# Longer rows for the high part of the residual: eight tiles at eight places in SBUF

## The chip, the cores and the metric

The kernel runs on one core of one Trainium2 chip. The metric is the device time of one execution in microseconds (us). The times of before and after are medians over several runs; a profile is taken of one execution. The engines are called as in the profile: PE is TensorE (PEld its weight loads), DVE is VectorE, ACT is ScalarE, POOL is GpSimd, SP is SyncE, which issues most DMAs.

## The reference

The reference is a trunk of two encoder layers on a sequence of 512 tokens of 1024 channels, all in float32. Cut to what matters:

```
for i in range(2):
    proj = x @ w_in[i]                        # (512, 1024) @ (1024, 5120)
    qa, ka, va, qb, kb, vb, gl = split(proj)
    oa = banded_attention(rope(qa), rope(ka), va, sink)          # window 128
    ob = mix of three dilated_attention(rope(qb), rope(kb), vb)  # dilations 1, 4, 16
    ga, gb = split(sigmoid(gl + b_gate))
    h = (ga * (oa @ w_branch_a) + gb * (ob @ w_branch_b)) @ w_out
    x = layer_norm(ALPHA * x + h)
    mlp = relu(x @ w_up) ** 2 @ w_down        # 1024 -> 4096 -> 1024
    ple = sigmoid(x @ w_ple_gate + b) * (p[i] @ w_ple)
    x = layer_norm(ALPHA * x + mlp + ple)
```

## The kernel before

The residual x lies transposed in SBUF for the whole program: channels on the 128 partitions, in eight tiles (k = 0 to 7) of 128 channels by 512 tokens. A float32 value is kept as two parts of the type float32r: a high part, made by ScalarE with a cast, and a low part, the rest, made by VectorE with a subtraction. For x these are the tiles xhi and xlo. Weights are split in the same way into whi and wlo (bhi and blo where a set is held longer, dhi and dlo in the down projection), after they were fetched to wst by DMA. A product of two such numbers is three matmuls (high by high, low by high, high by low), which add up in one bank of PSUM:

```
        def mm3(ps, w, i, x, start, stop, part=False):
            s = slice(i * P, (i + 1) * P)
            nc.tensor.matmul(ps, w[0][:, s], x[0], ...)    # L308: stationary whi, moving xhi
            nc.tensor.matmul(ps, w[0][:, s], x[1], ...)    # L309: stationary whi, moving xlo
            nc.tensor.matmul(ps, w[1][:, s], x[0], ...)    # L310: stationary wlo, moving xhi
```

The tile named first behind the arrow in a row of the profile is the moving operand, the one that is streamed through the array, 512 columns at most; the second is the stationary one, which a weight load has put there. mm3t (L314 to L316) is the same with the roles changed: 128 tokens of x are stationary, 512 columns of weights move.

Two lines make the residual's tiles, in the pool cp, which is the first on the left side of SBUF:

```
        xhi = cp.tile([P, KT, S], F32R, name="xhi")
        xlo = cp.tile([P, KT, S], F32R, name="xlo")
        X = [(xhi[:, k, :], xlo[:, k, :]) for k in range(KT)]
```

Each layer goes through these stages. The attention stage projects x by w_in, block after block of 128 output channels (8 tiles x 3 matmuls by mm3 each; start is the first four blocks together, in the second layer partly in halves of 256 tokens), and puts the small matmuls of attention between them: scores (sa L509, sb L504), transposes of the probabilities (pta, ptb, L472), sums over values (oa, ob, L513 and L514). A forecast in the program sets the order of TensorE's work there; elsewhere it is the order in which the code is written. The mixer's outputs go through gates, the branch projections (ya, yb) and the output projection (wo). Then come the layer norm, the transposes back (xTn L1032), and new xhi and xlo: ScalarE writes xhi at L1041, VectorE reads it at L1043 to make xlo. The gate of the embedding (pg) uses mm3t with x as the stationary operand. The up projection (ps_up) makes 32 blocks of 128 by mm3 from all eight tiles, in four quarters; between the quarters stands the down projection (dn L1156), which reads hidden activations and weights, not x. A second layer norm closes the layer.

xhi is read by TensorE in the projections by w_in, in the up projection (L308, L310, moving) and in the gate of the embedding (L314, L315, stationary). The tiles of the left pools stand behind xhi in SBUF: xlo and small vectors in cp, weights in wp, then, one after another, the attention stage's pool av, the pool yp of the layer's result y, and the pools np and qp. Pools of the right side (rp, hp, wb, rg) are laid out from the other end.

Of the kernel before, what the change touches and what calls it, by code (L numbers as in the profile page):

```python
# [11 lines left out]
F32R = mybir.dt.float32r  # L12
# [9 lines left out]
P = 128  # L22
S = 512
D = 1024
KT = 8
# [197 lines left out]
def build(nc, tc, plan, down, xT, xN, pT, wst, vec, rows, sink, cst, out):  # L223
# [3 lines left out]
    with ctx:  # L227
        cp = ctx.enter_context(tc.tile_pool(name="cp", bufs=1))
# [132 lines left out]
            return pss  # L361


        xhi = cp.tile([P, KT, S], F32R, name="xhi")
        xlo = cp.tile([P, KT, S], F32R, name="xlo")
        X = [(xhi[:, k, :], xlo[:, k, :]) for k in range(KT)]

# [1178 lines left out]
```

## Time and profile before

| what | value |
|---|---|
| median of 3 runs | 1506.17 us (1505.03 to 1506.38) |
| the profiled execution | 1504.93 us |
| its span, first to last instruction | 1503.2 us |
| granted TensorE clock | 0.998 |
| TensorE busy, matmuls | 1491.1 us (99%), 7242 |
| VectorE busy | 1044.7 us (69%) |
| ScalarE busy | 762.4 us (51%) |
| GpSimd busy | 255.1 us (17%) |

Shares are of the span. A busy time counts an instruction from its start to its end, and matmuls overlap, so a share of 99% says that TensorE hardly ever stands still, and nothing about how fast it goes while it works. That is read from the distance between the starts of neighbouring matmuls, in the rows in order of time.

### The profile page before, as it was taken

To read this page: it belongs to the slowest core of one execution; us is meant where nothing else is said; L and a number is where in the kernel's file an instruction comes from. 1 tells how busy PE (TensorE), PEld (TensorE's weight loads), DVE (VectorE), ACT (ScalarE), POOL (GpSimd) and SP (SyncE) were. 2 spreads that over 40 slices of the span, in tenths; PEclk is the share of its full clock that TensorE was granted. 3 is DMA by queue.
4 is the path that set the end of the run, shared out by engine and by line. 5 is a ranking of instruction groups with operands and counts; after the bars stand their busy time and mean duration, and the time that the engine had idled before them with its cause. 6 is when DMAs were issued, how large, how long until landed. Compare 5 with 4: busy or idle time off the path is not lost.

```text
span 1503.2 us, 19458 instructions
## 1 busy us (share of the span) xinstructions
PE 1491.1 (99%) x7242; PEld 1241.0 (83%) x7242; DVE 1044.7 (69%) x1796; ACT 762.4 (51%) x1256; POOL 255.1 (17%) x216
## 2 busy tenths in 40 slices
PE   9999999999999999999999999999999999999997
PEld 7888888888888888888888888888888888888886
DVE  6766675458577677677877666754685867777778
ACT  5777774344344443434458777643442544444344
POOL 1212211110021110213012122102100202111121
PEclk9999999999999999999999999999999999999999
DMA  7656564555523414142366666546755233241402
GB/s 263 151 135 153 136 160 124 186 160 154 182 60 94 127 57 154 42 141 84 97 203 140 141 148 143 152 135 167 239 153 182 70 113 112 84 127 54 139 18 70
DMA packets 58894, 197.41 MB, mean 131 GB/s; under 512 B 7440, under 2 KB 7984, under 8 KB 58800
## 3 DMA queue, kind: packets, MB, share of 16 engines
q1 hardware_dynamic: 47552, 159.08, 33.1%
q0 software_dynamic: 10256, 36.70, 13.2%
q8 instruction: 56, 0.92, 0.2%
q10 hardware_dynamic: 992, 0.39, 0.1%
q14 instruction: 38, 0.31, 0.1%
HBM read 161.46 MB, written 6.37 MB: 112 GB/s over the span
## 4 chain that ended last, share of the span: by engine, by line
PE 92%; DVE 4%; ACT 1%; DMA 1%; issue 0%; POOL 0%; SPq 0%; DVEq 0%; POOLq 0%; ACTq 0%
PE dn L1156 19%; PE ps_up L310 8%; PE ps_up L309 8%; PE ps_up L308 8%; PE wo L316 2%; PE wo L314 2%; PE wo L315 2%; PE pg L314 2%; PE pg L315 2%; PE pg L316 2%; PE sa L509 1%; PE pta L472 1%; PE sb L504 1%; PE ya L308 1%; PE ya L309 1%; PE ya L310 1%
## 5 line engine op out<-in xcount | busy, mean ns | idle before, releaser
L249 ACT CAST whi<-wst 128x1024 fp32r<-128x1024 f32 (+2 forms) x120 | 121.2, 1010 | 252.2 <-PE ps_up L309 102.7
L250 DVE TENSOR_TENSOR wlo<-wst,whi 128x1024 fp32r<-128x1024 f32 (+2 forms) x120 | 149.2, 1248 | 100.8 <-ACT whi L249 99.6
L1119 POOL TENSOR_TENSOR hr<-r 128x512 f32<-128x512 f32 x64 | 108.8, 1701 | 547.4 <-ACT r L1111 516.1
L310 PE MATMUL ps_up<-xhi,wlo 128*128 128x512 f32 x512 | 199.5, 390 | 0.0
L308 PE MATMUL ps_up<-xhi,whi 128*128 128x512 f32 x512 | 199.4, 390 | 0.0
L309 PE MATMUL ps_up<-xlo,whi 128*128 128x512 f32 x512 | 199.4, 390 | 0.0
L309 PEld LDWEIGHTS ps_up<-xlo,whi 128*128 128x128 f32 x512 | 96.2, 188 | 19.9
L308 PEld LDWEIGHTS ps_up<-xhi,whi 128*128 128x128 f32 x512 | 96.1, 188 | 19.9
L310 PEld LDWEIGHTS ps_up<-xhi,wlo 128*128 128x128 f32 x512 | 96.2, 188 | 19.9
L1172 DVE TENSOR_TENSOR y<-y,dn 128x512 f32<-128x512 f32 (+1 forms) x98 | 65.9, 672 | 62.9 <-PE dn L1156 62.8
L249 ACT CAST whi<-raw 128x1024 fp32r<-128x1024 f32 x56 | 58.0, 1053 | 96.0 <-PE ps_up L309 57.7
L249 ACT CAST dhi<-raw 128x1024 fp32r<-128x1024 f32 x56 | 58.6, 1050 | 85.9 <-PE dn L1156 57.3
L256 POOL DMA_DIRECT2D wlo<-wst x54 | 47.3, 876 | 246.0 <-ACT wlo L255 151.9
L1099 DVE TENSOR_TENSOR raw<-raw,raw 128x1024 f32<-128x1024 f32 x64 | 84.7, 1324 | 0.3
L250 DVE TENSOR_TENSOR wlo<-raw,whi 128x1024 fp32r<-128x1024 f32 x56 | 68.3, 1220 | 14.1 <-ACT whi L249 14.1
L254 ACT CAST whi<-wst 128x1024 fp32r<-128x1024 f32 x54 | 56.5, 1047 | 32.3 <-PE ps_start L309 4.3
L250 DVE TENSOR_TENSOR dlo<-raw,dhi 128x1024 fp32r<-128x1024 f32 x56 | 68.9, 1239 | 3.6 <-ACT dhi L249 3.6
L255 ACT ACTIVATE wlo<-whi 128x1024 fp32r<-128x1024 f32 x54 | 57.3, 1061 | 0.9
L1156 PE MATMUL dn<-wlo,smh 128*128 128x512 f32 (+1 forms) x130 | 51.1, 393 | 0.2
L1130 DVE TENSOR_TENSOR sml<-sr,smh 128x1024 fp32r<-128x1024 f32 x32 | 43.7, 1365 | 10.8 <-ACT smh L1129 10.8
L1156 PE MATMUL dn<-whi,smh 128*128 128x512 f32 (+1 forms) x130 | 50.4, 390 | 0.0
L1156 PE MATMUL dn<-whi,sml 128*128 128x512 f32 (+1 forms) x130 | 50.3, 387 | 0.0
(860 smaller groups left out, 4039.0 us busy)
## 6 DMA issues: line engine op xcount, KB each, us to landing
wst<-wst SPq DMA_DIRECT2D x187, 512.0 KB, 3.6
raw<-wst SPq DMA_DIRECT2D x64, 512.0 KB, 4.3
wlo<-wst POOLq DMA_DIRECT2D x54, 512.0 KB, 5.0
y<-rows POOLq DMA_DIRECT2D x12, 512.0 KB, 7.0
row<-rows SPq DMA_DIRECT2D x7, 512.0 KB, 5.2
R<-line SPq DMA_DIRECT2D x24, 128.0 KB, 3.8
wst<-wst SPq DMA_DIRECT2D x9, 256.0 KB, 2.9
xs<-xT SPq DMA_DIRECT2D x8, 256.0 KB, 6.8
```

What stands on the lines that cost most here:

```text
L249: nc.scalar.copy(hi, src)
L250: nc.vector.tensor_tensor(lo, src, hi.bitcast(F32), ALU.subtract)
L308: nc.tensor.matmul(ps, w[0][:, s], x[0], start=start, stop=False, skip_group_check=part)
L309: nc.tensor.matmul(ps, w[0][:, s], x[1], start=False, stop=False, skip_group_check=part)
L310: nc.tensor.matmul(ps, w[1][:, s], x[0], start=False, stop=stop, skip_group_check=part)
L314: nc.tensor.matmul(ps, x[0], w[0][:, c], start=start, stop=False)
L315: nc.tensor.matmul(ps, x[0], w[1][:, c], start=False, stop=False)
L316: nc.tensor.matmul(ps, x[1], w[0][:, c], start=False, stop=stop)
L1099: nc.vector.tensor_tensor(to, to, other, ALU.add)
L1119: nc.gpsimd.tensor_tensor(h.rearrange("p s t -> p (s t)"), r, r, ALU.mult)
L1156: nc.tensor.matmul(ps, a[:, k, tok], w[b][:, cols], start=first and not (k or m), stop=k == 3 and m == 2, skip_group_check=True)
L1172: return nc.vector.tensor_tensor(to, to, ps, ALU.subtract if n in (2, 4, 5) else ALU.add)
```

## The change

The rows of xhi, one for each tile k, become 16 elements (64 bytes) longer, and the program uses the first 512 of each. The tile takes 8 x 64 = 512 bytes more in each partition, so what lies behind it on the left side begins 512 bytes higher. xlo keeps its form.

```
-        xhi = cp.tile([P, KT, S], F32R, name="xhi")
+        xhi = cp.tile([P, KT, S + 16], F32R, name="xhi")[:, :, :S]
         xlo = cp.tile([P, KT, S], F32R, name="xlo")
         X = [(xhi[:, k, :], xlo[:, k, :]) for k in range(KT)]
```

In the built program xhi begins at byte 1664 of a partition, before and after, which is 128 modulo 512. Before, the tiles k = 0 to 7 all begin at 128 modulo 512; after, at 128, 192, 256, 320, 384, 448, 0 and 64. No instruction is added, taken away or moved on any engine, and each waits for the same semaphores as before.

## The prediction

> **What bounds the kernel now.** I read the page first, then the waits of TensorE, then the instructions that touch the changed tile, then rows in order of time to get the pace of the matmuls, which the page does not give.
>
> From the page: the first line of part 1, the clock row of part 2 and the first line of the chain.
>
> ```profile
> PE 1491.1 (99%) x7242; PEld 1241.0 (83%) x7242; DVE 1044.7 (69%) x1796; ACT 762.4 (51%) x1256; POOL 255.1 (17%) x216
> ...
> PEclk9999999999999999999999999999999999999999
> ...
> PE 92%; DVE 4%; ACT 1%; DMA 1%; issue 0%; POOL 0%; SPq 0%; DVEq 0%; POOLq 0%; ACTq 0%
> ```
>
> TensorE is busy 99% of the span, at the full clock, and carries 92% of the chain that ends last. The waits of TensorE confirm it: eight rows in all, of which these are the first and the last.
>
> ```profile
> PE out L1426 <- ACT y L1015: 1.5, 1, 1.5
> ...
> PE xTn L1032 <- DVE y L1019: 0.2, 1, 0.2
> ```
>
> So the kernel is as long as its matmuls take one after another, and an edit that adds no instruction can change the time in one way only: by changing how fast matmuls follow each other. How many can be touched is said by TensorE's instructions that read or write xhi, over the whole span, in one row (us, busy time, count, clock, DMA share, GB/s), and by the same tile's rows for the up projection and the gate of the embedding.
>
> ```profile
> 0.00:1503.20 1503.20, 819.44 (x2592) 1.00 0.47 131
> ```
>
> ```profile
> L308 PE MATMUL ps_up<-xhi,whi x512: 388/390/390, 419.3 to 1453.5; 128*128 128x512 f32 x171
> ...
> L314 PEld LDWEIGHTS pg<-bhi,xhi x128: 187/188/190, 368.3 to 1163.6; 128*128 128x128 f32 x128
> L314 PE MATMUL pg<-bhi,xhi x128: 388/390/477, 368.5 to 1163.8; 128*128 128x512 f32 x128
> L315 PEld LDWEIGHTS pg<-blo,xhi x128: 187/188/191, 368.5 to 1163.9; 128*128 128x128 f32 x128
> ...
> L1041 ACT ACTIVATE xhi<-xTn,vraw x48: 457/482/522, 361.9 to 1129.9; 128x256 fp32r<-128x256 f32 x48
> L1043 DVE SCALAR_TENSOR_TENSOR xlo<-xTn,vraw,xhi x48: 465/476/485, 363.0 to 1132.0; 128x256 fp32r<-128x256 f32 x48
> ```
>
> 2592 matmuls read xhi: 2 x 128 of them (L314, L315) as the stationary operand, the other 2336 (L308, L310) as the moving one. The 390 ns is the length of one matmul with its tail, which overlaps the next. The pace is the distance between starts, which rows in order of time show. Here are the first and the last of seven starts of the up projection, 512 columns each (start, us, line, operands):
>
> ```profile
> 1200.12 0.39 PE L309 MATMUL ps_up<-xlo,whi 128*128 128x512 f32 x1
> ...
> 1201.48 0.39 PE L309 MATMUL ps_up<-xlo,whi 128*128 128x512 f32 x1
> ```
>
> Six steps in 1.36 us are 226.7 ns each. The same for 21 starts of the second layer's first projections, 256 columns each:
>
> ```profile
> 765.11 0.28 PE L309 MATMUL ps_start<-xlo,whi 128*128 128x256 f32 x1
> ...
> 767.51 0.28 PE L308 MATMUL ps_start<-xhi,whi 128*128 128x256 f32 x1
> ```
>
> Twenty steps in 2.40 us are 120.0 ns each. 256 more columns cost 106.7 ns, so a column costs 0.417 ns and what is left, 226.7 - 512 x 0.417 = 13.3 ns, is paid once per matmul whatever its length. Those 13.3 ns are the only part of the pace that a place in memory could plausibly change.
>
> **The change, part by part.** (1) Instructions: none is added, removed or moved; built, both programs have the same instructions in the same order on all five queues, with the same waits on the same semaphores. Cost 0, and no cover is needed for it.
>
> (2) Places of xhi. In the built program before, xhi begins at byte 1664 of each partition and its rows are 2048 bytes long, so all eight tiles begin at 128 modulo 512. With rows of 2112 bytes they begin at 128, 192, 256, 320, 384, 448, 0 and 64. Tile 0 stays, seven of eight move: 2592 x 7/8 = 2268 matmuls. One nanosecond on each is 2.3 us. The weight tiles, xlo and everything else TensorE reads outside the attention stage begin at 128 modulo 512, before and after.
>
> No row of before has xhi elsewhere, so its price is bounded by the nearest rows: matmuls of the attention stage, where the tiles of pool av (q, k, the transposed probabilities) begin at 192 and the values at 448 modulo 512. First the scores (L509: moving k at 192, stationary q at 192) and the matmul behind them, then the weighted sums (L513, L514: moving at 192, stationary at 448) and the transpose behind them:
>
> ```profile
> 64.19 0.28 PE L509 MATMUL sa<-ql0ka,qhqa 128*128 128x256 f32 x1
> 64.31 0.28 PE L509 MATMUL sa<-qh1ka,qlqa 128*128 128x256 f32 x1
> 64.43 0.28 PE L509 MATMUL sa<-ql1ka,qlqa 128*128 128x256 f32 x1
> 64.55 0.40 PE L308 MATMUL ps_('kb', 0, 0)_721<-xhi,whi 128*128 128x512 f32 x1
> ...
> 65.94 0.39 PE L308 MATMUL ps_('kb', 0, 0)_721<-xhi,whi 128*128 128x512 f32 x1
> ...
> 67.30 0.28 PE L513 MATMUL oa<-ptha,vvva 128*128 128x256 f32 x1
> 67.42 0.28 PE L514 MATMUL oa<-ptla,vvva 128*64 128x256 f32 x1
> 67.54 0.28 PE L513 MATMUL oa<-ptha,vvva 128*128 128x256 f32 x1
> 67.65 0.28 PE L514 MATMUL oa<-ptla,vvva 128*64 128x256 f32 x1
> 67.77 0.49 PE L472 MATMUL pta<-ident,pa 128*128 128x128 f32 x3
> ```
>
> The scores step by 120 ns (64.19 to 64.55 in three): a moving operand at 192 costs the same as one at 128, at 256 columns. The weighted sums step by 0.47 / 4 = 117.5 ns, 2.5 ns less, with moving and stationary at different places; but half of these load only 64 columns of weights (the 128*64 of L514), so the place need not be the reason. The bound below: all 13.3 ns vanish, -13.3 x 2268 = -30.2 us. The bound above, from the slowest steady rows: L308 to L310 between 64.55 and 65.94 take 1.39 / 6 = 231.7 ns, 5.0 more than in the up projection, which would be +11.3 us. I take the row that is nearest in kind, the scores: same number type, same full 128 x 128 weights, only another place, difference 0.0 ns. Term: 0 us, ends -30.2 and +11.3.
>
> (3) xhi as stationary operand (L314, L315). Its load takes 188 ns and one starts every 226.7 ns, so some 39 ns lie free behind each; 256 x 7/8 = 224 loads are covered up to there. Term 0.
>
> (4) Writers and other readers of xhi. ScalarE writes it 48 times (482 ns) and VectorE reads it 48 times (476 ns) at the layer norms, and 8 times each at the start. The spread of those rows, 522 - 482 = 40 ns, on all 48 is 1.9 us, were none of it covered; but no row of TensorE's waits names L1041 or L1043, and matmuls of the embedding run meanwhile. Term 0, ends -1 and +1.9.
>
> (5) Everything behind xhi in the left pools (xlo, weights, attention tiles, y, the down projection's tiles) lies 512 bytes higher. The weights of before already stand at 0, 512, 1024 ... behind their start, in three buffers 4096 bytes apart, and the 512 matmuls of the L308 row above lie between 388 and 390 ns. Steps of 512 bytes show nothing. Term 0.
>
> The sum is 0 on the profiled execution, 1504.93 us (span 1503.2 and 1.7 around it), which lies 1.2 us under the median of the runs shown, 1506.17, and at the low end of their 1505.03 to 1506.38. I forecast the median, 1506.2. A measurement of this kernel can tell about 0.2%, 3.0 us, from no change; that is 1.3 ns on each of 2268 matmuls.
>
> [...] The trace has 226.7 ns between matmuls of 512 columns. [...]
>
> **The rivals.** *Faster: moving and stationary operand at the same place modulo 512 get in each other's way, and the change parts them.* For it: the 13.3 ns stand in every row in which both begin at 128, and the one place with two different starts (192 and 448) steps 2.5 ns less. Against it: scores with both at 192 step like the rest of 256 columns, and L514's narrow weights explain the shorter step as well. Worked out: 2.5 x 2268 = 5.7 us, 1500.5; with all 13.3 ns, 1476.
>
> *Slower: a moving operand that begins 64 bytes past a multiple of 128 needs one more fetch.* That is tiles 1, 3, 5 and 7, half of the 2592. For it: nothing that steps 512 columns in before begins so, and 512 columns are where the pace is tightest. Against it: 192 is such a place, and the scores pay nothing; the 231.7 ns of the attention stage come right behind short matmuls, with xhi at the same place as in the up projection, so they are no matter of place. Price: 5.0 ns x 1296 = 6.5 us, 1512.7; if all seven moved tiles pay, 11.3 us, 1517.5. It decides from 3.0 us / 1296 = 2.3 ns per matmul on.
>
> *The change does not do what it says.* The places follow from the built program, so this is excluded for xhi; what may hold is that no place matters, which is my forecast.
>
> **How the numbers follow.** No place matters: 0.70. Faster by the parting of the operands: 0.13, mostly at its small end, since the 2.5 ns are measured and the 13.3 are only the room there is. Slower by another fetch: 0.17, a little more than faster, since the only measured gain has another explanation, and tiles at 256, 320, 384, 0 and 64 have no row at all. The first case's own range is 1506.2 +- 3.0. The range that leaves out 2 in 10 takes in the small price of each rival, 1500.5 and 1512.7, to 1499.5 and 1513. The chances of faster, same and slower are those of the three cases.
>
> **What would show it.** In the profile after, the seven starts of the up projection again 1.36 us long whatever tile they begin with, and the L308, L309 and L310 rows of ps_up with one mean, prove term (2). If places matter, L308 and L310 part from L309, whose xlo stays at 128 modulo 512: by more for the odd tiles if it is the fetch, by the same for seven of eight if it is the parting. L314 and L315 against L316 show (3). A wait of TensorE on L1041 or L1043 would show (4) wrong, and the pace of L1156, which does not read xhi, shows (5). The forecast is wrong if a start at other than 128 or 192 costs or spares over 1.3 ns a matmul.

## The result, and the profile after

The changed kernel takes 1522.59 us (median of 4 runs, 1522.04 to 1523.08), the kernel before 1505.60 us (4 runs, 1504.87 to 1506.38). The ratio is 1.0112, with a 95% interval of 1.01 to 1.0125: 1.1% slower, and outside the forecast's range. The profiled execution after took 1523.08 us, its span 1521.2 us, at a granted clock of 0.999.

From the page of the kernel after, TensorE's part of the busy times, the clock row and the first line of the chain that ended last; then one answer of the waits of TensorE (waited for: us in all, times, longest), its first row:

```profile
PE 1509.5 (99%) x7242; PEld 1240.3 (82%) x7242; DVE 1045.4 (69%) x1796; ACT 762.5 (50%) x1256; POOL 251.6 (17%) x216
...
PEclk9999999999999999999999999999999999999999
...
PE 96%; DVE 2%; DMA 1%; ACT 0%; issue 0%; POOL 0%; SPq 0%; DVEq 0%; POOLq 0%; ACTq 0%
```

```profile
PE out L1426 <- ACT y L1015: 1.5, 1, 1.5
```

Waiting is not where the time went: the same 7242 matmuls, the same full clock, six waits of TensorE against eight before, and the same longest one of 1.5 us. TensorE's busy time is 18.4 us longer, and the span 18.0. The matmuls themselves go slower. Which ones is told by tiles. First TensorE's instructions on xhi over the span (us, busy time, count, clock, DMA share, GB/s), then the rows of the up projection and of the embedding's gate, and further down those of one operand pair of the down projection (ns min/median/max):

```profile
0.00:1521.20 1521.20, 829.19 (x2592) 1.00 0.46 130
```

```profile
L308 PE MATMUL ps_up<-xhi,whi x512: 389/393/400, 423.0 to 1471.3; 128*128 128x512 f32 x171
L309 PE MATMUL ps_up<-xlo,whi x512: 388/393/402, 423.2 to 1471.6; 128*128 128x512 f32 x171
L310 PE MATMUL ps_up<-xhi,wlo x512: 389/393/397, 423.4 to 1471.8; 128*128 128x512 f32 x171
```

```profile
L314 PE MATMUL pg<-bhi,xhi x128: 389/392/476, 371.5 to 1177.0; 128*128 128x512 f32 x128
L315 PE MATMUL pg<-blo,xhi x128: 389/393/397, 371.7 to 1177.2; 128*128 128x512 f32 x128
L316 PE MATMUL pg<-bhi,xlo x128: 388/392/398, 372.0 to 1177.5; 128*128 128x512 f32 x128
```

Before the change the rows of L309 and L316 were:

```profile
L309 PE MATMUL ps_up<-xlo,whi x512: 388/390/390, 419.5 to 1453.7; 128*128 128x512 f32 x171
```

```profile
L316 PE MATMUL pg<-bhi,xlo x128: 388/390/398, 369.0 to 1164.3; 128*128 128x512 f32 x128
```

And the down projection after:

```profile
L1156 PE MATMUL dn<-dhi,smh x130: 283/389/398, 479.9 to 1508.0; 128*128 128x512 f32 x126, 128*128 128x256 f32 x4
```

In the up projection a matmul lasted 388 to 390 ns; now its median is 393 and it goes up to 402. L309, whose stream xlo did not move, is as much longer as L308 and L310, and in the gate L316, which does not touch xhi, as much as L314 and L315. The down projection, which reads no x, has 389 (390 before). These lengths overlap; the loss is read from the starts in order of time:

```profile
1209.83 0.39 PE L308 MATMUL ps_up<-xhi,whi 128*128 128x512 f32 x1
...
1211.22 0.40 PE L308 MATMUL ps_up<-xhi,whi 128*128 128x512 f32 x1
...
1212.63 0.39 PE L308 MATMUL ps_up<-xhi,whi 128*128 128x512 f32 x1
```

From the first to the last of these are twelve steps, 2.80 / 12 = 233.3 ns each; before, it was 226.7. Adding up all distances from one start to the next in the two traces, by the tile that is written, shows where the 18.0 us went (worked out from the rows in order of time; the trace has starts to the nanosecond, the rows show them to ten):

```
                              matmuls   before, us   after, us   difference   ns each before, after
ps_up                           1536      348.16       357.38       +9.22       226.7   232.7
projections by w_in             1968      448.19       454.09       +5.90
  of these ps_g                  768      177.44       180.21       +2.77       231.0   234.6
pg (x stationary)                384       87.15        88.68       +1.53       227.0   230.9
dn (no x)                       1368      310.19       310.48       +0.29       226.7   227.0
wo (no x)                        384       87.06        87.05       -0.01       226.7   226.7
all else                        1602                                +1.1
```

16.7 of the 18.0 us lie in streams that read x, on either side of the array. In the up projection the distances behind L308, L309 and L310 depend on the tile k and repeat after four tiles, that is after 256 bytes (means over 64 blocks, ns):

```
k = 0   237.6 231.9 230.4      k = 4   239.2 232.5 230.8
k = 1   236.7 240.8 230.8      k = 5 to 7 as k = 1 to 3, within 1 ns
k = 2   231.7 225.8 228.4
k = 3   230.8 231.7 234.1      before: 226.4 to 226.8 in all places
```

### The profile page after: what moved, and what is told of

It reads as the page before. It is cut to its first block, busy times and chain, and to the rows that moved or that the text cites. A ratio compares the mean times of both kernels' runs of the same rounds, so it can differ in the third digit from the quotient of the medians.

```text
span 1521.2 us, 19458 instructions
## 1 busy us (share of the span) xinstructions
PE 1509.5 (99%) x7242; PEld 1240.3 (82%) x7242; DVE 1045.4 (69%) x1796; ACT 762.5 (50%) x1256; POOL 251.6 (17%) x216
## 4 chain that ended last, share of the span: by engine, by line
PE 96%; DVE 2%; DMA 1%; ACT 0%; issue 0%; POOL 0%; SPq 0%; DVEq 0%; POOLq 0%; ACTq 0%
PE dn L1156 19%; PE ps_up L309 8%; PE ps_up L308 8%; PE ps_up L310 8%; PE wo L314 2%; PE wo L316 2%; PE wo L315 2%; PE pg L314 2%; PE pg L315 2%; PE pg L316 2%; PE sb L504 1%; PE sa L509 1%; PE pta L472 1%; PE ya L308 1%; PE ps_start L308 1%; PE ps_start L309 1%
## 5 line engine op out<-in xcount | busy, mean ns | idle before, releaser
L308 PE MATMUL ps_up<-xhi,whi 128*128 128x512 f32 x512 | 202.5, 395 | 0.0
L309 PE MATMUL ps_up<-xlo,whi 128*128 128x512 f32 x512 | 201.9, 394 | 0.0
L310 PE MATMUL ps_up<-xhi,wlo 128*128 128x512 f32 x512 | 201.4, 393 | 0.0
L310 PEld LDWEIGHTS ps_up<-xhi,wlo 128*128 128x128 f32 x512 | 96.0, 188 | 23.6
L308 PEld LDWEIGHTS ps_up<-xhi,whi 128*128 128x128 f32 x512 | 96.1, 188 | 22.9
L309 PEld LDWEIGHTS ps_up<-xlo,whi 128*128 128x128 f32 x512 | 96.1, 188 | 22.4
L314 PE MATMUL pg<-bhi,xhi 128*128 128x512 f32 x128 | 50.3, 393 | 0.0
```

The lines of the kernel that those rows point to most:

```text
L308: nc.tensor.matmul(ps, w[0][:, s], x[0], start=start, stop=False, skip_group_check=part)
L309: nc.tensor.matmul(ps, w[0][:, s], x[1], start=False, stop=False, skip_group_check=part)
L310: nc.tensor.matmul(ps, w[1][:, s], x[0], start=False, stop=stop, skip_group_check=part)
L314: nc.tensor.matmul(ps, x[0], w[0][:, c], start=start, stop=False)
```

## The experiments

Below, the difference means the place where the weights begin, minus the place where the stream begins, modulo 256 bytes. Before the change it is 0 for every long stream outside the attention stage (all at 128). Weights of one up projection block are 512 bytes for each k, so the difference doesn't depend on k unless x moves. All places are read from the built programs. "Pace" is the mean distance of starts. Experiments 4, 5 and 7 to 12 are one execution each; their paces come from its trace.

**1. All xhi tiles moved alike.** xhi begins at 192 modulo 512 in all eight tiles; xlo and the weights stay at 128.

```
-        xhi = cp.tile([P, KT, S], F32R, name="xhi")
+        xhi = cp.tile([P, KT * S + 128], F32R, name="xhi")[:, 16:16 + KT * S].rearrange("p (k s) -> p k s", k=KT)
```

> All eight tiles of xhi begin at 192 modulo 512, one like the other; xlo, weights and everything else stay at 128. Collision theory (a matmul's stream and the weight load that runs beside it get in each other's way, by the difference of their places): two of three streams stand 64 bytes from the weights, so the pace of the up projection leaves 226.7 ns, alike for all eight tiles; some +2 to +9 ns on two of three, 1511 to 1520 us. Change-of-place theory (a stream whose place differs from that of the matmul before it loses time): the streams go high, low, high, so two of three steps change place; about as slow as the changed kernel, 1516 to 1523 us. Absolute theory (a start at an odd multiple of 64 costs): L308 and L310 slower, L309 at 226.7 ns, 1511 to 1520 us.

1525.24 us against 1505.48, ratio 1.0133 (1.0118 to 1.0148), above the ranges of all three theories. The up projection's pace is 233.3 ns, and all three lines are slow: the mean distances behind L308, L309 and L310 are 233.3, 235.8 and 230.8. So L309 does not stay at 226.7, as the absolute theory had it. Rows of the gate in this kernel:

```profile
L314 PE MATMUL pg<-bhi,xhi x128: 394/398/477, 372.3 to 1178.8; 128*128 128x512 f32 x128
L315 PE MATMUL pg<-blo,xhi x128: 390/392/398, 372.6 to 1179.0; 128*128 128x512 f32 x128
L316 PE MATMUL pg<-bhi,xlo x128: 392/398/399, 372.8 to 1179.3; 128*128 128x512 f32 x128
```

The gate, where xhi is stationary, slows down too: its medians are 392 to 398 ns against 390 before. One place for all tiles, only another than that of weights and xlo, costs more than the change's eight places (1525.24 us against 1522.59). So the number of places isn't what costs.

**2. Four tiles moved by 256 bytes.** Tiles 4 to 7 of xhi begin at 384, the rest stays.

```
-        xhi = cp.tile([P, KT, S], F32R, name="xhi")
+        xhi = cp.tile([P, KT * S + 128], F32R, name="xhi")
-        X = [(xhi[:, k, :], xlo[:, k, :]) for k in range(KT)]
+        X = [(xhi[:, k * S + k // 4 * 64:][:, :S], xlo[:, k, :]) for k in range(KT)]
```

> Tiles 0 to 3 of xhi stay at 128 modulo 512, tiles 4 to 7 begin 256 bytes further on, at 384. In the changed kernel tiles k and k + 4 had the same steps, so the period should be 256 bytes: all three theories then give 226.7 ns for every tile and 1505.6 us. If the period is 512 bytes, tiles 4 to 7 of the up projection step differently from tiles 0 to 3, and the time goes up by some us (half of the 17 us, 1514).

1505.33 us, ratio 0.9999 (0.9989 to 1.0008); pace 226.67 ns.

```profile
L308 PE MATMUL ps_up<-xhi,whi x512: 388/390/390, 419.1 to 1452.9; 128*128 128x512 f32 x171
```

The row is that of before. For xhi 256 bytes are a whole period here, as the table by k said.

**3. xhi and xlo moved alike.** Both streams begin at 192, the weights at 128: the difference is 192 in every matmul, and no place changes from one stream to the next.

```
-        xhi = cp.tile([P, KT, S], F32R, name="xhi")
-        xlo = cp.tile([P, KT, S], F32R, name="xlo")
+        xhi = cp.tile([P, KT * S + 16], F32R, name="xhi")[:, 16:16 + KT * S].rearrange("p (k s) -> p k s", k=KT)
+        xlo = cp.tile([P, KT * S + 112], F32R, name="xlo")[:, 0:0 + KT * S].rearrange("p (k s) -> p k s", k=KT)
```

> xhi and xlo both begin at 192 modulo 512 in all tiles; the weights stay at 128. Collision theory: every stream stands 64 bytes from the weights, so all three lines of the up projection leave 226.7 ns, alike for all tiles; 1512 to 1530 us. Change-of-place theory: no two streams in a row differ in place, 226.7 ns everywhere, 1505.6 us. Absolute theory: all three lines slower, as with collision.

1514.29 us, ratio 1.006 (1.0043 to 1.0077). The up projection's pace is 229.0 ns, in a rhythm of three, 229, 232, 226, that repeats.

```profile
1358.66 0.40 PE L308 MATMUL ps_up<-xhi,whi 128*128 128x512 f32 x1
...
1360.72 0.40 PE L308 MATMUL ps_up<-xhi,whi 128*128 128x512 f32 x1
```

Nine steps in 2.06 us are 228.9 ns each. That refutes the theory that only a change of place between streams costs: here nothing changes, and the pace is 229.0 ns against 226.7. In the gate, where x is stationary and the difference is 64 instead of 192, the pace is 233.6. The same two places with the roles exchanged have another price, 6.6 ns against 2.3.

**4. A sweep of the weights' place.** Streams stay at 128; the up projection's weights of block m begin later by 0, 64, 128, 192, 32, 96, 256 and 384 bytes (m = 0 to 7). To make room, two buffers hold the incoming weights instead of three here and in experiments 5, 7, 9 and 12; with that second change in them their whole times (1537 to 1544 us) aren't compared, only the pace.

```
+            o = (0, 16, 32, 48, 8, 24, 64, 96)[plan[c][0][1][2]] if plan[c][0][1][0] == "up" else 0
-            hi, lo = (pool.tile([P, 1024], F32R, ...) for e in ("hi", "lo"))
+            hi, lo = (pool.tile([P, 1152 if pool is wp else 1024], F32R, ...)[:, o:o + 1024] for e in ("hi", "lo"))
```

> xhi and xlo stay as before; the weight tiles of the up projection begin 0, 32, 64, 96, 128, 192, 256 or 384 bytes further on, by the block m of 128 outputs (24 matmuls each, 64 blocks in all). To make room, the buffers for incoming weights are two and not three, which may cost some us elsewhere. Collision theory: the pace inside a block depends on its shift, 226.7 ns at 0, 256 and 384 less 256, other values at 64, 128 and 192. Change-of-place theory and absolute theory for the moving operand: 226.7 ns in all blocks, since the streams never change place.

The steady pace, as the mean of eleven distances in the second half of each block (a rhythm need not fit eleven evenly, so a mean can be off by half a nanosecond or so):

```
shift of weights, bytes     0     32     64     96    128    192    256    384
ns each                   226.7  233.5  233.5  234.0  233.7  229.2  226.7  232.9
```

Moving the weights does what moving the streams did: 192 gives experiment 3's rhythm of 229, 232 and 226, and 256 is free. The block at 256 shows something new. It follows one that is out of step, and its first ten distances are 233, 236, 224, 231, 235, 228, 232, 231, 227, 226 ns, and 227 from there on.

**5. The same in steps of 8 bytes**, 0 to 248 (shift 64 q + 8 m for quarter q, block m).

```
+            o = (plan[c][0][1][1] * 16 + plan[c][0][1][2] * 2) if plan[c][0][1][0] == "up" else 0
```

> xhi and xlo as before; the weight tile of each block of the up projection begins 8 bytes further on than that of the block before it in number (0, 8, ... 248 bytes, two blocks of 24 matmuls for each). Incoming weights have two buffers and not three. Collision theory: the pace is a function of the shift alone: 226.7 ns at 0, about 229 at 192, 233 to 234 at 32, 64, 96 and 128 as in the coarse sweep, and from 128 to 248 a way back down. If 226.7 ns is itself a remainder of collisions, some shift lies under it. If only whole lines of 64 bytes count, shifts 8 to 56 step all alike.

Steady pace in ns:

```
  0 226.7    8 230.6   16 233.4   24 230.8   32 233.5   40 233.5   48 233.4   56 233.3
 64 233.5   72 233.3   80 231.7   88 233.4   96 233.9  104 233.3  112 233.4  120 226.7
128 233.0  136 233.3  144 233.0  152 230.8  160 233.6  168 233.0  176 230.4  184 232.1
192 229.2  200 230.8  208 233.3  216 226.7  224 233.2  232 231.0  240 226.7  248 233.3
```

Most shifts cost 4 to 7 ns, even 8 bytes; 120, 216 and 240 cost nothing, and no shift is faster than 0. A smooth effect of distance is ruled out, and so is one that counts only whole lines of 64 bytes, since 8 to 56 are not alike. None of these 32 places beats the kernel before.

At 128 this run and experiment 4 read the same places in different rhythms. In experiment 4, behind a block shifted by 96, the steps are 238 and 229 in turn (233.3 as a mean of twelve); here, behind the down projection, seven steps of 241, 232, 231, 232, 228, 230 and 233 repeat (232.4). So the places alone don't fix the rhythm: the mean is 233.3 ns in one run and 232.4 in the other, and what ran just before is different.

**6. The attention stage put in step.** The kernel before, with q, k, values and probabilities at 128 modulo 256, where the projections have their operands.

```
-            sk = av.tile([P, 8], F32, tag="sk", name=f"sk{l}", bufs=1)
+            sk = av.tile([P, 56], F32, tag="sk", name=f"sk{l}", bufs=1)[:, :8]
```

> The kernel before with 192 unused bytes ahead of the attention tiles, so that q, k, probabilities and values begin at 128 modulo 256 like xhi and the weights, and not at 192. Nothing else changes. Collision theory: the 230 to 241 ns steps of the projections behind each piece of attention come from weights and streams 64 bytes apart at the switch, and go; about 10 us stand above 226.7 ns in that stage, of which 4 to 8 go: 1497 to 1501 us. Rival (TensorE's queue has to fill again behind short matmuls): no change, 1504.5 to 1506.5.

1505.56 us against 1505.07, ratio 1.0003 (0.9994 to 1.0012): no change, where a gain was expected. The pace of ps_g, the projections between the attention's pieces, went from 231.0 to 231.2 ns. What slows these projections in the kernel before isn't the place of the attention's tiles. The result is the one that the rival gives, but nothing here shows that a queue is the reason.

**7. Every matmul's own operands matched.** The kernel after, with xlo's rows and the up projection's rows of weights 64 bytes longer too, so that stream and weights of tile k both stand at 128 + 64 k.

```
+        xlo = cp.tile([P, KT, S + 16], F32R, name="xlo")[:, :, :S]
...
-            s = slice(i * P, (i + 1) * P)
+            s = slice(i * w[2], i * w[2] + P)      # w[2] = 144 in the up projection
```

> The changed kernel, with the rows of xlo and of the up projection's weights longer by 64 bytes too, so that the stream and the weights of each of its matmuls stand at the same place, whatever the tile. Incoming weights have two buffers and not three. If a stream collides with the load of its own weights' place: 226.7 ns on all three lines. If it collides with the load that runs beside it, which is the next matmul's: two of three pairs are at the same place and the third (L310, beside the load for the next tile) stands 64 bytes off, so the mean lies between 227.5 and 232. Rival (change of place from one matmul to the next): 232 or more.

The pace is 231.6 ns, not 226.7. A difference of 0 within each matmul isn't enough when the common place changes after every third one. The first form of the collision theory falls. The second (the load that runs beside) and the rival aren't separated: 231.6 lies in the range of the one and just under that of the other. The loss isn't on L310 alone, though: the mean distances behind L308, L309 and L310 are 230.3, 231.6 and 232.8.

**8 and 10. Narrower weight loads.** In the kernel after (8) and before (10), loads and outputs of the up projection have 128, 64, 32 and 96 columns in quarters 0 to 3, from tile 1 on; the rest of each block is left out.

```
+                            mm3(ps[:(128, 64, 32, 96)[q] if k else P], w, k, x, ..., (128, 64, 32, 96)[q] if k else P)
```

> The changed kernel; from the second tile of each block on, the up projection loads and computes only the first 128, 64, 32 or 96 columns of weights in its quarters 0 to 3 (the rest of the outputs is left with the first tile's part). Collision with the weight load: the fewer columns are loaded beside a stream of 512, the less it loses: 232.7 ns with 128 columns, some 229 with 96, 222 with 64, 218 with 32. Rival (the stream's own place is what costs): 232.7 ns in all quarters.

> The kernel before; from the second tile of each block on, the up projection loads and computes only the first 128, 64, 32 or 96 columns of weights in its quarters 0 to 3 (the rest of the outputs keeps the first tile's part). If the 13.3 ns that each stream of 512 columns pays are collisions with the load beside it, fewer columns cost less: 226.7, some 220, 217 and 223 ns. If they are a fixed price of a matmul, 226.7 ns in all quarters.

```
columns loaded          128     64     32     96
pace after, ns         232.5  229.1  231.9  232.1
pace before, ns        226.7  229.6  231.6  230.0
```

Means over each block behind its first tile. None of the four forecasts came out. In the traces of before and after, each load of the up projection starts 2 to 5 ns behind the start of the stream before its own. If a load got in the way of the stream beside it in proportion to what it reads, narrower loads would be faster. Before the change they are slower, although a load of 32 columns takes some 110 ns there and one of 128 takes 188. This form of the theory falls. Whether the narrower load or the narrower output is what costs isn't separated.

**9. Streams and weights moved together.** xhi and xlo at 192, weights by block at places that give differences of 0, 192, 32, 64, 120, 256, 216 and 128 modulo 256.

```
+            o = (16, 0, 24, 32, 46, 80, 6, 48)[plan[c][0][1][2]] if plan[c][0][1][0] == "up" else 0
```

> xhi and xlo both at 192 modulo 512, as in the third experiment; the weight tiles of the up projection are moved by block so that they stand 0, 192, 32, 64, 120, 256, 216 and 128 bytes behind xhi and xlo (m = 0 to 7). Incoming weights have two buffers and not three. If the difference between stream and weights decides: the paces of the two sweeps come back at the same differences, 226.7 ns at 0, 256, 120 and 216, 229 at 192, 233 to 234 at 32, 64 and 128. If the place itself decides: 226.7 ns where the weights stand at 128 (difference 192), and something else where both stand at 192.

```
difference     0    192     32     64    120    256    216    128
ns each      226.7 229.2  233.5  233.1  226.7  226.7  232.1  231.8
```

Two rows of a block with everything at 192:

```profile
607.41 0.39 PE L308 MATMUL ps_up<-xhi,whi 128*128 128x512 f32 x1
...
609.45 0.39 PE L308 MATMUL ps_up<-xhi,whi 128*128 128x512 f32 x1
```

Nine steps in 2.04 us are 226.7 ns each, where experiment 3, with the same streams and only the weights at 128, has 2.06 us. With both at 192 the pace is that of both at 128. So 192, 64 past a multiple of 128, is no worse a start than 128 (226.7 ns with both operands there): it is the difference that counts. It agrees with the sweeps to 0.4 ns at six of eight points, and at 128 it repeats experiment 5's rhythm of seven. At 216 it is 5.4 ns worse than there. Three things are different at that point and aren't told apart: the place of the streams, the difference modulo 512 (472 here, 216 there), and the block before, which is out of step here (32) and in step there (240).

**11. Shorter streams.** The kernel before, the eight blocks of each quarter with 512, 508, 504, 496, 480, 448, 384 and 256 columns from tile 1 on; the rest is left out.

```
+                            n = (512, 508, 504, 496, 480, 448, 384, 256)[m] if k else S; mm3(ps[:, :n], w, k, [t[:, :n] for t in x], ...)
```

> The kernel before; from the second tile of each block on, the up projection streams only the first 512, 508, 504, 496, 480, 448, 384 or 256 columns in blocks m = 0 to 7 (the other tokens keep the first tile's part). A fixed price of 13.3 ns gives 226.7, 225.0, 223.3, 220.0, 213.3, 200.0, 173.3 and 120.0 ns. A grid of 13.3 ns on which streams start gives 226.7 ns for 508, 504 and 496 too, and 213.3 for 480.

Steady pace, again as the mean of eleven distances in the second half of each block:

```
columns              512    508    504    496    480    448    384    256
ns each              226.7  228.4  226.7  223.3  217.0  206.7  173.3  120.0
columns / 2.4 + 13.3 226.7  225.0  223.3  220.0  213.3  200.0  173.3  120.0
```

The prediction's 13.3 ns a matmul hold for 256, 384 and 512 columns alone, of the lengths tried here. The others, with all places in step, pay 3.3 to 6.7 ns more, which is the size of what a shift costs. Neither forecast, a fixed price or a grid, gives all of them. The 2.4 of the last row is the prediction's pace of 256 columns in 106.7 ns.

**12. Rarer changes of the common place.** Experiment 7 with tiles in another order in each quarter. The common place changes by +64 bytes after six matmuls, after three, never, and by 64 bytes after twelve.

```
+                        KS = ((0, 4, 1, 5, 2, 6, 3, 7), range(8), (0, 4) * 4, (0, 4, 0, 4, 1, 5, 1, 5))[q]
+                        for n, k in enumerate(KS):
+                            mm3(ps, w, k, X[k], n == 0, n == KT - 1)
```

> As the kernel in which rows of xhi, xlo and of the up projection's weights are all 64 bytes longer, so that every matmul finds its own stream and its own weights at one place, but the eight tiles come in another order in each quarter, so that the common place changes by 64 bytes after every six matmuls (quarter 0: tiles 0 4 1 5 2 6 3 7), every three (quarter 1: 0 to 7), never (quarter 2: 0 and 4 in turn, four times) and every twelve (quarter 3: 0 4 0 4 1 5 1 5). Quarters 2 and 3 leave tiles out and use others several times. Both theories give 231.6 ns for quarter 1, as measured, and 226.7 for quarter 2. Theory A, each change has a price of its own: 4.9 ns on three matmuls are 14.7 ns for each change, so 226.7 + 14.7 / 6 = 229.1 ns in quarter 0 and 226.7 + 14.7 / 12 = 227.9 ns in quarter 3. Theory B, a change upsets a rhythm that needs some ten matmuls to settle, as the first blocks after a shift did: about 231 ns in quarter 0 and 229 to 230.5 in quarter 3, with the late ones of the twelve back at 226.7. The whole time is not compared: as in that kernel, two buffers hold the incoming weights instead of three.

The pace is 230.3, 231.6, 226.7 and 228.8 ns in quarters 0 to 3. Twelve rows with tiles 0 and 4, from 1470.32 to 1473.05, and twelve with 1 and 5, from 1473.05 to 1475.81:

```profile
1470.32 0.39 PE L308 MATMUL ps_up<-xhi,whi 128*128 128x512 f32 x1
...
1473.05 0.39 PE L308 MATMUL ps_up<-xhi,whi 128*128 128x512 f32 x1
...
1475.81 0.39 PE L308 MATMUL ps_up<-xhi,whi 128*128 128x512 f32 x1
```

2.73 / 12 is 227.5 ns and 2.76 / 12 is 230.0. One by one, as means over the blocks of quarter 3:

```
tiles 0, 4 (behind 1, 5):  229 232 230 227 227 227 227 227 227 227 227 226
tiles 1, 5 (behind 0, 4):  228 229 233 236 224 231 236 228 233 231 227 226
```

Theory B is borne out in kind: one step of +64 bytes upsets ten matmuls, in the order of lengths that the block at 256 showed in experiment 4, and then the pace is back. A step back by 64 upsets three. In size neither theory is met: quarter 3's 228.8 lies between A's 227.9 and B's 229 to 230.5, since the step back is cheap, and quarter 0's 230.3 between A's 229.1 and B's 231.

## Why the prediction was wrong, point by point

**(1) Instructions, 0.** Right: 7242 matmuls before and after, and no wait of TensorE longer by more than 0.6 us.

**(2) Places of xhi, 0 with ends -30.2 and +11.3.** This is the step that failed: that a tile of x at another place costs nothing. It measured +15.1 us in the up projection and the projections by w_in, beyond its upper end. The row taken as "nearest in kind", the scores at 120 ns with both operands at 192, shows that a common place of 192 costs nothing at 256 columns, and experiment 9 confirms that at 512 (226.7 ns). It says nothing of operands that part, and the change parts them. Every stream of 512 columns in the kernel before has a difference of 0; the row that had one (weighted sums, 192 against 448) has 256 bytes, which experiment 2 shows to be a whole period for xhi (226.67 ns). That this was "the one place with two different starts" is not so: the transposes of the probabilities have ident at 128 and pa at 448, which is 64 apart modulo 256. But these streams have 128 columns, and their steps, mostly 107 to 110 ns, hardly change in experiment 6, where the difference is 0 (108 to 110). So no row of the kernel before showed what the change adds. The count was wrong as well. Of the 2268 moved matmuls those of tile 4 moved by a whole period, while L309 and L316, whose operands stay, pay as much as their neighbours; experiments 4 and 12, where a step upsets eight to ten matmuls, are a likely reason. The upper end came from rows behind attention pieces, at 231.7 ns; times 2268 it gave +11.3.

How two causes add up is seen in the up projection. With a steady difference alone the change's four places would cost what experiments 4 and 5 show for weights at 0, 192, 128 and 64: 226.7, 229.2, 233.3 and 233.5 ns, 230.7 as a mean on L308 and L310, and 226.7 on L309, so 229.3 in all. Measured are 232.7. The other 3.4 ns I put down to the changes of place between streams, which experiments 7 and 12 show to cost 3.6 to 4.9 ns when they come after every sixth or third matmul; that these two prices add is argued, not shown. In experiment 1 the same sum (229.2 on two of three lines, 226.7 on L309) gives 228.4 and leaves 4.9 of the measured 233.3.

**(3) xhi as stationary operand, 0.** Wrong by 1.5 us, on all three lines of the gate. The cover was there: a weight load took 188 ns before, and so it does after, as the group in the up projection shows (busy us, mean ns, idle before):

```profile
L308 PEld LDWEIGHTS ps_up<-xhi,whi 128*128 128x128 f32 x512 | 96.1, 188 | 22.9
```

In both traces each load of the up projection ends at least 34 ns ahead of the stream that needs it, and so does each load of the gate but one. So the streams don't wait for their weights: it is their own pace that stretches. That a load was covered in time did not keep the place of its operand from counting.

**(4) Writers and readers, 0.** Right:

```profile
L1041 ACT ACTIVATE xhi<-xTn,vraw x48: 465/486/521, 364.9 to 1142.0; 128x256 fp32r<-128x256 f32 x48
```

```profile
L1043 DVE SCALAR_TENSOR_TENSOR xlo<-xTn,vraw,xhi x48: 469/478/485, 366.0 to 1144.1; 128x256 fp32r<-128x256 f32 x48
```

Medians of 486 and 478 ns against 482 and 476, 48 each: 0.3 us in all, and no wait of TensorE names either line.

**(5) 512 bytes more for the rest, 0.** Right: dn at 227.0 and wo at 226.7 ns, although both lie 512 bytes higher.

**The rivals.** *Slower* had the sign right, by another mechanism. A fetch more for odd tiles would leave L309 alone, make tiles 2 and 6 free and make experiment 9's first column slow; all three are refuted (L309 steps 232.6 ns after the change, tile 2 231.7 and 228.4 on L308 and L310, and that column 226.7). *Faster* named the right pair of operands, and the effect is the reverse: the same place is the good case, 226.7 ns. Moving only where one operand begins takes the pace from 226.7 to between 229 and 234 ns at 28 of the 31 shifts of experiment 5. No stage and no steady block of 512 columns in the tables here has a mean under 226.7.

**What stays open** is what inside the chip makes the rhythm: why 120, 240 and, in one of two runs, 216 are free, why narrower loads are slower in experiment 10, and why a step of +64 bytes takes ten matmuls and one of -64 takes three in experiment 12. That the places of the two operands change the pace is shown (226.7 to 234.0 ns in experiments 4 and 5), that lengths do so too (up to 6.7 ns above the fixed price in experiment 11), and that a place left behind still shows in the next ten matmuls (224 to 236 ns in experiment 12). That the reads of the two operands collide is shown by no run, and the simple forms of that explanation (own weights, amount loaded) fell in experiments 7, 8 and 10. No kernel here that does the same work beats the one before.

## What to carry to other kernels

When TensorE streams 512 float32r columns back to back, try one place modulo 256 bytes for all its operands, stationary and moving, and pad rows and small tiles ahead of them by multiples of that: here 64 bytes of difference either way cost 0.6% of the time in experiment 3 and 1.3% in experiment 1. Read the pace from distances of starts, since the share of busy time (99% before and after), the longest wait (1.5 us) and the loads (188 ns) looked the same when it went from 226.7 to 232.7 ns. And when a term is priced from the nearest row, ask whether that row has the thing that changes (here, a difference between two places) or only the new value in both.

## What was not expected of the hardware

- At 512 columns the steps of the up projection before, where all places agree, are 225 to 228 ns, and 226 or 227 in 1371 of 1536. A pace of 226.7 ns also came at a few other differences (120 and 240, and 216 in experiment 5 alone). Other differences gave repeating rhythms: two steps (235, 232) at a shift of 32 in experiment 4, three (229, 232, 226) at 192 in experiments 3 and 4.
- The same places gave two rhythms: at 128, two steps of 238 and 229 ns behind one block (experiment 4) and seven steps of 228 to 241 behind another (experiment 5).
- A disturbance outlasts its cause: in experiment 12, after one step of +64 bytes in place, ten matmuls of 512 columns step by 224 to 236 ns although all that they read is in step.
- In experiment 11, 480 columns take 217.0 ns and 448 take 206.7, while 384 take 173.3: the last 64 of 448 columns cost 33.4 ns, the first 64 beyond it 20.0.
- In experiment 10, narrower weights and outputs, which aren't told apart, slowed streams of 512 columns: 226.7 ns at 128 columns, 231.6 at 32.
